# Vectors and weights laid out by partition in memory, an early tanh, and one count of landings for two DMA queues

## The chip, the core and the metric

The kernel runs on one core of a Trainium2 chip. The core has five engines with instruction streams of their own: TensorE (PE, with its weight loads in a row PEld), VectorE (DVE), ScalarE (ACT), GpSimd (POOL) and SyncE (SP). SP and ACT also issue DMAs: each has a queue in its own stream, and all of them are carried out by the same 16 DMA engines. The metric is device time in microseconds (us) of one execution; smaller is better.

## The reference, cut to what matters

One layer of a streaming encoder on 2048 prompt rows and 64 sample rows of width 1024, in float32:

```python
mod = silu(c) @ w_ada + b_ada                       # six vectors per sequence, from c
sh1, sc1, gt1, sh2, sc2, gt2 = split(mod, 6)
h = rms_norm(x, norm1_g) * (1 + sc1) + sh1
z = h @ w_in                                        # glu_a | glu_b | q | k | v | g_conv | g_attn
u = glu_a * sigmoid(glu_b)
conv_out = silu(layer_norm(depthwise31(u) + b_dw)) @ w_conv_out
q, k = rms_norm(q) * q_norm_g, rms_norm(k) * k_norm_g        # per head of 64
o = softmax(q k^T / 8 + rel_bias, in a band of 9 chunks of 64) v
x = x + gt1 * ((sigmoid(g_conv) * conv_out + sigmoid(g_attn) * (o @ w_attn_out)) @ w_o)
h2 = rms_norm(x, norm2_g) * (1 + sc2) + sh2
x = x + gt2 * ((silu(gate) * up) @ w_ffn_out)       # gate, up = split(h2 @ w_ffn_in)
```

Outputs are x of both sequences, the last 30 rows of u, and the new rows of k and v. The sample sequence also reads cached rows (`cache_k`, `cache_v`, `cache_conv`).

## The kernel before, in words

**Precision and slabs.** Each float32 operand of a matmul is split into a high part (`whi`, `hh`, `part_h`; an ACT copy to a shorter format) and a low part (`wlo`, `hl`, `part_l`; a subtraction on DVE or POOL), and a product is three matmuls: high by high, high by low, low by high (`mm3`). Weights come from memory in slabs of 512 KB into staging tiles (`wst`, three of them), are split into `whi` and `wlo`, and some split slabs are stored (`w_din_h`, `w_dqkv_h`, ...) to be read again in a later block.

**Stages.** The rows are worked on in four blocks of about 512. A block goes through q, k, v, four conv stages and the gates "g"; the attention of a block (scores `sc`, softmax in `pr` and `sm`, its transposed parts `ph` and `pl`, output `po`) runs beside the conv and gate products. In each gate step ACT makes a tile `gate` and stores it to `g_d` by a DMA in its own queue. The 31 taps of the convolution are DVE instructions on `y`. A second phase in three blocks does the two out-projections and the feed-forward network.

**The start** (`first_rows`, `setup`, `first_block`). The sums for c @ w_ada need `cl`, which is made from c by one tanh on ACT, and the slabs `wmod` of w_ada, four of which fit (`Slabs`). Before, c and the other vectors are read as rows (`r`) and turned into columns by PE. The rows `x_t` are squared on ACT, scaled by DVE after a power on POOL, turned by PE (`turn`, into `pt`), scaled by the modulation (`h`), split into `hh` and `hl`, and multiplied with the first slabs of w_in for q (`ps`).

**What sets the order.** No instruction is issued when the code calls it: `Plan.do` records it, and `Plan.flush` plays all engines forward with a table of costs and writes the instructions in the order of the planned starts. A DMA is planned no earlier than the landing of the eighth DMA before it (`Plan.room` with `self.flight`); which ready instruction comes first on an engine goes by a due time that is worked out backwards from the order of PE, with 8000 ns added to a DMA's latency.

**Semaphores of DMAs.** In the built program the DMAs of SP and ACT together take eight semaphores in turn, so a DMA of either queue waits at its issue until the eighth DMA before it, of whichever queue, has landed. What stands behind it in the stream of its engine waits with it, on ACT the activations too.

All instructions that are recorded in the plan carry line 388 in the profile, where `flush` issues them, so they are told apart by the names of their tiles.

Of the kernel before, what the change touches and what calls it, by code (L numbers as in the profile page):

```python
# [9 lines left out]
F32 = mybir.dt.float32  # L10
# [148 lines left out]
class Plan:  # L159
# [145 lines left out]
    def flush(self, last=False):  # L305
# [106 lines left out]
    def place(self, o, s):  # L412
# [534 lines left out]
def streaming_layer(ctx: ExitStack, tc: tile.TileContext, I, O):  # L947
# [7 lines left out]
    w_in, w_ada = I["w_in"][0], I["w_ada"][0]  # L955
    w_co, w_ao, w_o = I["w_conv_out"][0], I["w_attn_out"][0], I["w_o"][0]
    w_fi, w_fo = I["w_ffn_in"][0], I["w_ffn_out"][0]
# [3 lines left out]
    ck = I["cache_k"][0, 0].rearrange("t h d -> t (h d)")  # L961
# [31 lines left out]
    dve.memset(mhalf, -0.5)  # L993
# [7 lines left out]
    cols = const.tile([P, 76], F32, name="cols")  # L1001
    gates_c = const.tile([P, 2, 2, KT], F32, name="gates_c")
    lnh = const.tile([P, 8], F32, name="lnh")
    wd = const.tile([P, 4, TAPS], F32, name="wd")
    gqk = const.tile([P, 2], F32, name="gqk")
    gk = const.tile([P, HD], F32, name="gk")
    hist = const.tile([P, 4, HIST], F32, name="hist")
    hist_s = const.tile([P, 4, HIST], F32, name="hist_s")
# [5 lines left out]
    def source(key):  # L1014
        kind, a = key[0], key[1]
        by_col = lambda w, c0, n=P: w[:, c0 : c0 + n].rearrange("(k p) n -> p k n", p=P)
        if kind == "mod":
            if len(key) == 5:
                r = slice(512 * key[3], 512 * key[3] + 512)
                return [by_col(w_ada[r], a * D + key[2] * 2 * P, 2 * P)], 4, 2 * P  # L1020
            r = slice(256 * key[3], 256 * key[3] + 256)
            return [by_col(w_ada[r], a * D + key[2] * 512, 512)], 2, 512
        if kind == "qkv":
            r = slice(2 * key[2] * P, 2 * key[2] * P + 2 * P)
            return [by_col(w_in[r], 2 * CONV + 512 * a, 512)], 2, 512
        if kind == "in" and len(key) == 3:
            return [by_col(w_in[512 * key[2] : 512 * key[2] + 512], a, 2 * P)], 4, 2 * P
        if kind == "in":
            return [by_col(w_in, a)], KT, P
        if kind == "fi":  # L1030
            return [by_col(w_fi, a)], KT, P
        if kind == "up":
            return [
                sum_d[f][int(op[1]) - 1] if op[0] == "s"
                else by_col(w_fi[512 * (op != "a11") : 512 * (op != "a11") + 512], f * P + FFN * (op == "a22"))
                for f, op in key[1:]
            ], 4 * len(key) - 4, P
        if kind == "ca":
            return [by_col(w_co, a * P), by_col(w_ao, a * P)], KT, P
# [52 lines left out]

    plan.on = True
# [17 lines left out]
    def load_vectors():  # L1111

        r0 = temp("r0", (16, P))
        r1 = temp("r1", (76, P))
        by_row = lambda a: a.rearrange("(r c) -> r c", c=P)
        scalar.dma_start(r0[0:8], by_row(I["c_prompt"][0]))
        scalar.dma_start(r0[8:16], by_row(I["c_sample"][0]))
        yield r0, r1
        o = 0
        for name in ("norm1_g", "norm2_g", "b_dw", "conv_ln_g", "conv_ln_b", "b_ada"):  # L1120
            a = by_row(I[name][0])
            sync.dma_start(r1[o : o + a.shape[0]], a)
            o += a.shape[0]
        yield

    def setup():
        r0, r1 = first_vectors
        pt = ps_g.tile([P, 512], F32, tag="gp", name="pt")
# [17 lines left out]
        def vectors():  # L1146
            pt = ps_g.tile([P, 512], F32, tag="gp", name="pt")
            pe.transpose(pt[:, :76], r1, ident[:76, :76])
            dve.tensor_copy(cols, pt[:, :76])
# [5 lines left out]
        def taps():  # L1155
            for i in range(2):
                for j, g in enumerate((I["q_norm_g"], I["k_norm_g"])):
                    scalar.dma_start(gqk[HD * i : HD * i + HD, j : j + 1], g.rearrange("o d -> d o"))
            scalar.dma_start(gk, I["k_norm_g"].to_broadcast([P, HD]))
            cc = wk.tile([HIST, CONV], F32, tag="pr", name="cc", bufs=8)  # L1160
            scalar.dma_start(cc, I["cache_conv"][0, 0])
            r2 = wk.tile([TAPS, CONV], F32, tag="pr", name="r2", bufs=8)
            scalar.dma_start(r2, I["w_dw"][0])
            yield
            pt = ps_a.tile([P, 4, P], F32, tag="o", name="pt")
            for c in range(4):
                pe.transpose(pt[:, c, :TAPS], r2[:, c * P : (c + 1) * P], ident[:TAPS, :TAPS])
                pe.transpose(pt[:, c, 64 : 64 + HIST], cc[:, c * P : (c + 1) * P], ident[:HIST, :HIST])
            dve.tensor_scalar(wd, pt[:, :, :TAPS], 0.5, None, ALU.mult)
            dve.tensor_scalar(hist_s, pt[:, :, 64 : 64 + HIST], 2.0, None, ALU.mult)  # L1170
# [66 lines left out]
    def first_rows():  # L1237
        places = ((wa, "x", 3), (wa, "x", 3), (wa, "x", 3), (wk, "kk", 1), (wk, "q2", 1))
        queues = (sync, sync, scalar, sync, scalar)
        return [load_x(*tl, *place, q) for tl, place, q in zip(token_tiles(*PBLOCKS[0]), places, queues)]  # L1240

    def first_block(xs):
# [5 lines left out]
        def scale_rows(a, b):  # L1248
            for x_t, (t, n) in list(zip(xs, tiles))[a:b]:
                r = square(x_t, n)  # L1250
                dve.tensor_scalar(x_t[:n], x_t[:n], r, None, ALU.mult)

        def modulation(ct):
# [4 lines left out]
            with behind(pe.last.ins):  # L1258
# [88 lines left out]
    def store_kq(src, n, dst, col, g=None):  # L1347
# [4 lines left out]
        stream.after("act", "pe")  # L1352
        hi, lo = parts(shape=(P, 4, P))
# [60 lines left out]
    def cached_kv():  # L1414
        rows_ = [(src, j) for j in range(CACHE // P) for src in (ck, cv)]
        ts = []
        for i, (src, j) in enumerate(rows_):
            for src_, j_ in rows_[len(ts) : i + 2]:
                t = temp("cache")
                sync.dma_start(t, src_[j_ * P : (j_ + 1) * P])  # L1420
# [3 lines left out]
            if src is ck:  # L1424
                store_kq(t, P, k_d, j * P)
# [501 lines left out]
    vectors_ = load_vectors()  # L1927
    first_vectors = next(vectors_)
    M = Slabs(sync, scalar, wa, stream, list(mod_order()), source, 4)
    M.fill()  # L1930
    next(vectors_)
# [644 lines left out]
    "x_prompt", "x_sample", "c_prompt", "c_sample", "cache_conv", "cache_k", "cache_v", "norm1_g", "norm2_g",  # L2576
    "w_ada", "b_ada", "w_in", "w_dw", "b_dw", "conv_ln_g", "conv_ln_b", "w_conv_out", "q_norm_g", "k_norm_g",
    "rel_bias", "w_attn_out", "w_o", "w_ffn_in", "w_ffn_out",
# [4 lines left out]
]  # L2583

# [17 lines left out]
```

## Time and profile before

| | |
|---|---|
| median of three runs | 2958.19 us (2957.11 to 2959.2) |
| the profiled execution | 2954.55 us, its span 2952.7 us |
| PE busy | 2897.3 us, 98% of the span |
| DVE, ACT, POOL busy | 2056.5, 1361.9 and 1152.6 us |
| data moved by DMA | 628.06 MB, 213 GB/s over the span |

The span is the time from the first to the last instruction of the profiled execution. PE has work in 98% of it; the other 55.4 us are spread over a few places, which a list of waits names together with what ended each. "granted clock" (PEclk) is the share of full speed at which TensorE's clock ran in a stretch.

### The profile page before, as it was taken

Reading aid. Unit: us, or ns where it says so; the run is one execution under the profiler, and the core shown is the slowest. Engines: PE = TensorE matmul, PEld = TensorE weight load, DVE = VectorE, ACT = ScalarE, POOL = GpSimd, SP = SyncE. Lnnn points to the kernel's source line nnn. Section 1 sums busy time; section 2 is a strip of 40 time slices with the busy share of each in tenths; the row PEclk is TensorE's granted clock in tenths of the full one; section 3 lists DMA queues with packets and bytes.
Section 4 is the critical chain, followed back from the end, with each engine's and each line's share of the span. In section 5 each row is a group of like instructions: output and inputs, shape, how many; then the busy total and the mean of one; then the engine's idle time right before and its main releaser. Section 6 shows DMA issues by size and latency. Waiting matters only on the chain.

```text
span 2952.7 us, 44886 instructions
## 1 busy us (share of the span) xinstructions
PE 2897.3 (98%) x16241; PEld 2590.4 (88%) x16241; DVE 2056.5 (70%) x3628; ACT 1361.9 (46%) x2459; POOL 1152.6 (39%) x752
## 2 busy tenths in 40 slices
PE   7999999999999999989999999999999999999999
PEld 4899888888888888878888899999999999999998
DVE  5887788668867885577666745666666557576666
ACT  3345633662464356554444345544444355444442
POOL 0201310111011002544566452366666742465667
PEclk9999999999999999999999999999999999999999
DMA  9988999988886987975444876333333965333333
GB/s 293 300 296 289 300 308 317 297 261 315 278 280 201 314 259 237 312 258 169 145 143 143 265 248 225 108 117 97 105 122 111 335 221 185 97 104 104 115 110 123
DMA packets 467725, 628.06 MB, mean 213 GB/s; under 512 B 36277, under 2 KB 314665, under 8 KB 467502
## 3 DMA queue, kind: packets, MB, share of 16 engines
q1 hardware_dynamic: 453456, 605.58, 62.9%
q10 hardware_dynamic: 14045, 19.60, 1.9%
q8 instruction: 128, 2.10, 0.3%
q14 instruction: 96, 0.78, 0.1%
HBM read 476.53 MB, written 148.54 MB: 212 GB/s over the span
## 4 chain that ended last, share of the span: by engine, by line
PE 89%; DVE 4%; ACT 2%; DMA 2%; issue 1%; POOL 1%; SPq 0%; ACTq 0%; DVEq 0%; POOLq 0%
PE ps L388 59%; PE pd L388 16%; PE pw L388 6%; PE po L388 2%; PE sc L388 2%; PE ptp L388 2%; PE pt L388 1%; PE pa L388 1%; ACT whi L388 1%; DVE wlo L388 1%; DMA wst<-in_w_in 1%; DVE y L388 0%; POOL wlo L388 0%; DVE pw L388 0%; POOL ws L388 0%
## 5 line engine op out<-in xcount | busy, mean ns | idle before, releaser
L388 PE MATMUL ps<-t,whi 128*128 128x384 f32 (+1 forms) x2112 | 501.0, 322 | 8.9 <-ACT t L388 5.4
L388 POOL TENSOR_TENSOR wlo<-wst,whi 128x1024 fp32r<-128x1024 f32 (+1 forms) x160 | 365.2, 2291 | 292.9 <-ACT whi L388 243.8
L388 ACT ACTIVATE whi<-wst 128x1024 fp32r<-128x1024 f32 (+1 forms) x264 | 256.8, 976 | 292.0 <-PE ps L388 115.4
L388 PE MATMUL ps<-b,whi 128*128 128x384 f32 (+1 forms) x1584 | 381.9, 326 | 5.4 <-DVE t L388 2.2
L388 PEld LDWEIGHTS ps<-t,whi 128*128 128x128 f32 x2112 | 368.8, 188 | 15.4 <-ACT t L388 5.6
L388 DVE SCALAR_TENSOR_TENSOR y<-u,wd,y 128x512 f32<-128x512 f32 (+1 forms) x480 | 371.0, 775 | 7.8
L388 DVE TENSOR_TENSOR acc<-acc,pd 128x512 f32<-128x512 f32 (+1 forms) x482 | 324.4, 685 | 55.4 <-PE pd L388 49.7
L388 PE MATMUL ps<-hh,whi 128*128 128x512 f32 (+2 forms) x992 | 362.4, 366 | 0.0
L388 PE MATMUL ps<-hh,wlo 128*128 128x512 f32 (+2 forms) x992 | 346.6, 350 | 0.0
L388 PE MATMUL ps<-hl,whi 128*128 128x512 f32 (+2 forms) x992 | 346.1, 349 | 0.0
L388 PE MATMUL ps<-t,wlo 128*128 128x384 f32 (+1 forms) x1056 | 339.2, 322 | 0.0
L388 PE MATMUL pd<-whi,hid 128*128 128x512 f32 (+1 forms) x956 | 307.1, 391 | 0.0
L388 PEld LDWEIGHTS ps<-b,whi 128*128 128x128 f32 x1584 | 278.5, 189 | 11.6 <-DVE v L388 2.9
L388 PE MATMUL ps<-b,wlo 128*128 128x384 f32 (+1 forms) x792 | 257.3, 325 | 0.0
L388 ACT ACTIVATE pr<-pr,sm 128x640 f32<-128x640 f32 (+4 forms) x272 | 199.4, 746 | 119.8 <-DVE sm L388 114.5
L388 POOL TENSOR_TENSOR t<-t,mhalf 128x1 f32<-128x1 f32 (+3 forms) x68 | 85.9, 1270 | 425.5 <-DVE t L388 403.0
L388 PEld LDWEIGHTS pd<-whi,hid 128*128 128x128 f32 (+1 forms) x956 | 174.8, 183 | 40.9 <-ACT whi L388 0.2
L388 PEld LDWEIGHTS ps<-hh,wlo 128*128 128x128 f32 x992 | 187.4, 189 | 22.2 <-issue 0.9
L388 PEld LDWEIGHTS ps<-hh,whi 128*128 128x128 f32 x992 | 188.1, 190 | 18.4 <-issue 2.0
L388 PEld LDWEIGHTS ps<-hl,whi 128*128 128x128 f32 x992 | 188.4, 190 | 15.1 <-issue 1.2
L388 PEld LDWEIGHTS ps<-t,wlo 128*128 128x128 f32 x1056 | 198.5, 188 | 0.1
L388 POOL TENSOR_TENSOR wlo<-ws,whi 128x512 fp32r<-128x512 f32 x96 | 123.0, 1300 | 186.1 <-ACT whi L388 186.1
(232 smaller groups left out, 6297.6 us busy)
## 6 DMA issues: line engine op xcount, KB each, us to landing
whi<-w_din_h SPq DMA_DIRECT2D x72, 512.0 KB, 6.0
wlo<-w_din_l SPq DMA_DIRECT2D x72, 512.0 KB, 7.7
wst<-sum_d SPq DMA_DIRECT2D x132, 256.0 KB, 2.9
wfo<-in_w_ffn_out SPq DMA_DIRECT2D x64, 512.0 KB, 3.3
wmod<-in_w_ada SPq DMA_DIRECT2D x46, 512.0 KB, 6.1
sum_d<-ws SPq DMA_DIRECT2D x88, 256.0 KB, 2.6
wst<-in_w_ffn_in SPq DMA_DIRECT2D x84, 256.0 KB, 3.3
wst<-in_w_in SPq DMA_DIRECT2D x40, 512.0 KB, 8.9
```

Of the source, the lines that this page charges most:

```text
L388: f(*args, **kw)
```

## The change

It has four parts.

1. **Layout.** The host hands over the weights with the data of each slab contiguous for each partition (4 KB for one partition of a slab of 512 KB), all vectors as one tile of 128 x 92 with a column for each vector of 128 (`vec`), the taps, conv history and gains of q and k as one tile of 128 x 310 (`small`), and the cached k rows already turned. This only rearranges, repeats and joins arrays. Six loads of vectors, two of c, and seven small loads in `taps` become two loads; 18 transposes on PE and the copies behind them go; the two loads of a slab of conv and attention output weights (`ca`) become one.
2. **Start.** ACT issues the load of `vec` first, and a tanh of a constant right behind it, so that the table of functions is loaded while it lands. All slabs and all rows x are issued by SP; before, ACT issued two slabs and two rows. The square of a row is one instruction of 1024 elements, whose discarded result goes to the PSUM tile that `turn` uses first, instead of two of 512.
3. **Planner's flight.** `flight` is one list for both queues, as the semaphores are.
4. **Planner's due times.** 12000 ns in place of 8000 ns is added to a DMA's latency.

```diff
-        self.clock, self.pools, self.flight = 0.0, 0, {e: [] for e in ('sp', 'act')}
+        self.clock, self.pools, self.flight = 0.0, 0, []
...
-            lat = o.lat + self.HOP + (o.occ + o.size + 8000.0 if o.size else 0)
+            lat = o.lat + self.HOP + (o.occ + o.size + 12000.0 if o.size else 0)
...
-        if o.size and len(self.flight[o.engine]) > 7:
-            s = max(s, self.flight[o.engine][-8] + self.HOP)
+        if o.size and len(self.flight) > 7:
+            s = max(s, self.flight[-8] + self.HOP)
...
-            self.flight[o.engine].append(o.end)
+            self.flight.append(o.end)
...
-                return [by_col(w_ada[r], a * D + key[2] * 2 * P, 2 * P)], 4, 2 * P
+            return [I["ada_1"][a, key[2], key[3]]], 4, 2 * P
...
-            return [by_col(w_co, a * P), by_col(w_ao, a * P)], KT, P
+            return [I["w_ca"][a]], KT, P
...
+    scalar.dma_start(vec, I["vectors"])
+    act.activation(mhalf[:, 7:], eps_t, AF.Tanh)
+    dve.memset(mhalf, -0.5)
     plan.on = True
...
-        pe.transpose(pt[:, :16], r0, ident[:16, :16])
-        cc = wk.tile([P, 16], F32, tag="c0")
-        dve.tensor_copy(cc, pt[:, :16])
+        cc = vec[:, :16]
...
-            pe.transpose(pt[:, :76], r1, ident[:76, :76])
-            dve.tensor_copy(cols, pt[:, :76])
...
-                pe.transpose(pt[:, c, :TAPS], r2[:, c * P : (c + 1) * P], ident[:TAPS, :TAPS])
-                pe.transpose(pt[:, c, 64 : 64 + HIST], cc[:, c * P : (c + 1) * P], ident[:HIST, :HIST])
...
-        queues = (sync, sync, scalar, sync, scalar)
-        return [load_x(*tl, *place, q) for tl, place, q in zip(token_tiles(*PBLOCKS[0]), places, queues)]
+        return [load_x(*tl, *place) for tl, place in zip(token_tiles(*PBLOCKS[0]), places)]
...
-                r = square(x_t, n)
+                ssq = wk.tile([P, 2], F32, tag="ssq", name="ssq", bufs=3)
+                junk = ps_a.tile([P, 2 * 512], F32, tag="s", name="junk")
+                act.activation(junk[:n], x_t[:n], AF.Square, accum_out=ssq[:n, :1])
+                r = rsqrt_mean(wk, ssq[:n, :1], n, 1, D)
...
-            if src is ck:
-                store_kq(t, P, k_d, j * P)
+            if src == "k":
+                store_parts(t.rearrange("p (h t) -> p h t", h=4), P, k_d, j * P)
...
-    M = Slabs(sync, scalar, wa, stream, list(mod_order()), source, 4)
+    M = Slabs(sync, sync, wa, stream, list(mod_order()), source, 4)
...
+    a["ada_1"] = ada[:, : 2 * D].reshape(2, 4, P, 2, 4, 2 * P).transpose(3, 4, 0, 2, 1, 5)
+    a["w_gates"] = w_in[:, 2560:].reshape(2, 4, P, 8, 2 * P).transpose(3, 0, 2, 1, 4)
+    a["w_up"] = a["w_ffn_in"][0].reshape(KT, P, 2 * NF, P).transpose(2, 1, 0, 3)
```

The parts 3 and 4 change the order of instructions on all engines through the first phase and the beginning of the second. Two places are shown.

The first is ACT's stream from its first instruction, before. `r` holds the vector c, `rv` the table of relative biases, `t` the tanh of c, and `junk` the squares of the rows `x_t`:

```order
L388 DMA r_200<-in_c_prompt 8x128
L388 DMA r_200<-in_c_sample 8x128
L388 DMA wmod<-in_w_ada 128x4x256 x2
L388 DMA x_t<-in_x_prompt 128x1024 x2
L388 DMA rv<-in_rel_bias 8x257
L388 ACT_TABLE_LOAD
L388 ACTIVATE t<-t 128x16
L388 ACTIVATE junk,ssq<-x_t 64x512 x2
L388 ACTIVATE junk,ssq<-x_t 128x512 x8
L388 ACTIVATE whi<-wst 128x1024
```

And the same place in the changed kernel:

```order
L242 DMA vec<-in_vectors 128x92
L242 ACT_TABLE_LOAD
L242 ACTIVATE mhalf<-eps_t 128x1
L388 ACTIVATE t<-vec 128x16
L388 DMA rv<-in_rel_bias 8x257
L388 ACTIVATE junk,ssq<-x_t 64x1024
L388 ACTIVATE junk,ssq<-x_t 128x1024 x4
L388 ACTIVATE whi<-wst 128x1024
```

The tanh `t` moved from behind seven DMAs to behind one, and the load of the table from behind them to the place right after that one.

The second place is ACT's stream in the gates of block 0, beside the third head's scores, before. `pr` are the exponentials of the scores, 128 to 512 wide by chunk, `gate` the gate tiles, `whi` the high part of a slab:

```order
L388 ACTIVATE pr,sm<-pr,sm 128x256
L388 ACTIVATE gate<-ps 128x288
L388 ACTIVATE whi<-wst 128x1024
L388 ACTIVATE pr<-pr,sm 128x256
L388 ACTIVATE gate<-ps 128x288
L388 DMA g_d<-gate 128x288
L388 ACTIVATE pr,sm<-pr,sm 128x384
```

The same head's place in the changed kernel:

```order
L388 ACTIVATE pr,sm<-pr,sm 128x256
L388 ACTIVATE whi<-wst 128x1024
L388 ACTIVATE pr<-pr,sm 128x256
L388 ACTIVATE whi<-wst 128x1024
L388 ACTIVATE gate<-ps 128x288
L388 ACTIVATE pr,sm<-pr,sm 128x384
```

Between the exponentials of two chunks of one head stood one split of a slab, and now stand two; the store of a gate moved behind the next exponential. The loads of these slabs on SP's queue before, up to the first store of an attention output, `o_d` (`vv` are value rows, `w_din` stored slabs, `out` an output of the convolution state):

```order
L388 DMA vv<-v_d 128x4x128
L388 DMA out<-cc 30x128
L388 DMA wst<-in_w_in 128x4x256
L388 DMA w_din_1_h<-whi 128x1024
L388 DMA w_din_1_l<-wlo 128x1024
L388 DMA wst<-in_w_in 128x4x256
L388 DMA w_din_0_h<-whi 128x1024
L388 DMA vv<-v_d 128x2x128
L388 DMA vv<-v_d 64x128
L388 DMA w_din_0_l<-wlo 128x1024
L388 DMA o_d<-part_h 128x512
```

And in the changed kernel:

```order
L388 DMA vv<-v_d 128x4x128
L388 DMA wst<-in_w_gates 128x1024
L388 DMA w_din_1_h<-whi 128x1024
L388 DMA w_din_1_l<-wlo 128x1024
L388 DMA w_din_0_h<-whi 128x1024
L388 DMA w_din_0_l<-wlo 128x1024
L388 DMA vv<-v_d 128x2x128
L388 DMA vv<-v_d 64x128
L388 DMA out<-cc 30x128
L388 DMA o_d<-part_h 128x512
```

The last slab ahead of the output store is now issued six places ahead of `vv` 64x128 instead of three, and the conv state's store behind it.

More of the change, by code (lines that the diff above doesn't have):

```diff
@@ L1155, in taps @@
         def taps():
[L1156 to L1163, printed above, removed]
-            yield
-            pt = ps_a.tile([P, 4, P], F32, tag="o", name="pt")
-            for c in range(4):
-                pe.transpose(pt[:, c, :TAPS], r2[:, c * P : (c + 1) * P], ident[:TAPS, :TAPS])
-                pe.transpose(pt[:, c, 64 : 64 + HIST], cc[:, c * P : (c + 1) * P], ident[:HIST, :HIST])
-            dve.tensor_scalar(wd, pt[:, :, :TAPS], 0.5, None, ALU.mult)
-            dve.tensor_scalar(hist_s, pt[:, :, 64 : 64 + HIST], 2.0, None, ALU.mult)
+            scalar.dma_start(small, I["small"])
+            yield
+            dve.tensor_scalar(wd, wd, 0.5, None, ALU.mult)
+            dve.tensor_scalar(hist_s, hist_s, 2.0, None, ALU.mult)
         return vectors, taps, begun
@@ L1256, in modulation @@
             cs = [slice(c6 * 2 * P, (c6 + 1) * 2 * P) for c6 in range(2)]
-            with behind(pe.last.ins):
+            with behind(pe.last.ins) if ct else nullcontext():
                 for c6, c in enumerate(cs):
@@ L1414, in cached_kv @@
     def cached_kv():
-        rows_ = [(src, j) for j in range(CACHE // P) for src in (ck, cv)]
+        rows_ = [(src, j) for j in range(CACHE // P) for src in ("k", "v")]
         ts = []
@@ L2575 @@
 _INS = [
-    "x_prompt", "x_sample", "c_prompt", "c_sample", "cache_conv", "cache_k", "cache_v", "norm1_g", "norm2_g",
-    "w_ada", "b_ada", "w_in", "w_dw", "b_dw", "conv_ln_g", "conv_ln_b", "w_conv_out", "q_norm_g", "k_norm_g",
-    "rel_bias", "w_attn_out", "w_o", "w_ffn_in", "w_ffn_out",
+    "x_prompt", "x_sample", "cache_v", "rel_bias", "w_o", "w_ffn_out", "vectors", "small", "cache_k_t", "ada_1",
+    "ada_2", "w_qkv", "w_gates", "w_glu", "w_up", "w_ca",
 ]
@@ L2592 @@
     arrays, ins = {}, {}
-    for name in _INS:
-        a = np.ascontiguousarray(inputs[name])
+    for name, a in laid_out(np, inputs).items():
         arrays[f"in_{name}"] = a
```

74 lines of the change are left out of this document (34 added, 40 removed).

## The prediction

> **What bounds the kernel now.** I read the busy times first, then the waits of PE, then a table of stretches, and last the order of time at the places that these name.
>
> ```profile
> span 2952.7 us, 44886 instructions
> ...
> PE 2897.3 (98%) x16241; PEld 2590.4 (88%) x16241; DVE 2056.5 (70%) x3628; ACT 1361.9 (46%) x2459; POOL 1152.6 (39%) x752
> ...
> PE pa L388 <- DVE cl L388: 8.4, 1, 8.4
> PE sc L388 <- DVE sm L388: 8.1, 4, 3.2
> PE ps L388 <- ACT t L388: 5.4, 1, 5.4
> PE pt L388 <- DMA r<-in_c_sample: 4.8, 1, 4.8
> ```
>
> PE is idle for 2952.7 - 2897.3 = 55.4 us, and no matmul product is taken away. So the change can bring what is in those 55.4 us, the work of the transposes, and full clock where it runs slow. The waits (total, times, longest) put the largest pieces at the start (`cl`, `r`), in the attention (`sc`) and at the beginning of the feed-forward network (`t`).
>
> **The start.** In order of time (start, duration, instruction; in brackets the idle time before):
>
> ```profile
> 0.73 1.00 SPq L388 DMA_DIRECT2D wmod<-in_w_ada  x2
> ...
> 1.70 0.97 ACTq L388 DMA_DIRECT2D wmod<-in_w_ada  x2
> ...
> 6.10 0.34 SPq L388 DMA_DIRECT2D r<-in_b_ada  x1
> ...
> 11.09 0.30 ACTq L388 DMA_DIRECT2D rv<-in_rel_bias  x1
> ...
> 11.42 1.28 ACT L388 ACT_TABLE_LOAD   x1 [11.42 <-DMA wmod<-in_w_ada]
> 12.71 0.22 ACT L388 ACTIVATE t<-t 128x16 f32<-128x16 f32 x1
> 12.84 0.61 ACT L388 ACTIVATE junk<-x_t 64x512 f32<-64x512 f32 x1
> ...
> 13.40 3.64 PE L388 MATMUL pa<-wmod,cl 128*32 128x256 f32 x32 [8.38 <-DVE cl L388]
> ...
> 16.33 0.40 SPq L388 DMA_DIRECT2D wst<-in_w_in  x1
> ...
> 18.55 0.15 DVE L388 TENSOR_SCALAR t<-ssq 128x1 f32<-128x1 f32 x1
> ...
> 18.79 0.56 POOL L388 TENSOR_TENSOR t<-t,mhalf 128x1 f32<-128x1 f32 x1 [3.63 <-DVE t L388]
> ...
> 19.39 0.75 DVE L388 TENSOR_SCALAR x_t<-x_t,t 128x1024 f32<-128x1024 f32 x1 [0.68 <-POOL t L388]
> ...
> 25.41 0.67 DVE L388 TENSOR_SCALAR h<-pt,A,B 128x384 f32<-128x384 f32 x1
> ...
> 26.66 0.34 DVE L388 TENSOR_SCALAR h<-pt,A,B 128x64 f32<-128x64 f32 x1 [0.57 <-PE pt L388]
> ...
> 27.03 0.58 ACT L388 ACTIVATE hh<-h 128x448 fp32r<-128x448 f32 x1 [5.27 <-DVE h L388]
> ...
> 27.66 1.54 PE L388 MATMUL ps<-whi,hh 128*64 128x512 f32 x3 [1.04 <-ACT hh L388]
> ...
> 30.41 1.41 PE L388 MATMUL pt<-ident,x_t 64*128 64x64 f32 x5
> ...
> 32.18 2.09 PE L388 MATMUL pa<-wmod,cl 128*32 128x256 f32 x32
> ```
>
> The load of `rv` stands in ACT's stream ahead of the table load and the tanh. It waits for a semaphore that the first slab on ACT's queue holds, so the tanh runs only at 12.71 and the squares only from 12.84, although c was there by 4.8 us (the wait on `r`). The first product `ps` starts at 27.66; from then on PE has work.
>
> The load of `wst` at 16.33 waits for the last row x, so by then four slabs of 512 KB, four rows of 512 KB and one of 256 KB, 4.46 MB, are in.
>
> **Step 1, the start of the changed kernel.** Now c comes with `vec`, and the table is loaded meanwhile. I take 5 us for its landing (4.8 for c), and 5.4 for `cl`. The sums then go at the pace of the slabs, which come before the rows in one queue: 2.1 MB. The rate is read from a stretch in which only slabs and rows moved (columns: PE, PEld, DVE, ACT, POOL busy, granted clock, DMA share, GB/s):
>
> ```profile
> 12.00:14.00 2.00, 0.60 (x8) 0.37 (x12) 0.47 (x3) 1.99 (x6) 0.21 (x1) 1.00 1.06 374
> ```
>
> At 374 GB/s from 2 us on the fourth slab lands near 8 us, so modulation is ready before the rows and leaves the path. The last row lands between 2 + 4.46/0.374 = 13.9 and 16.3 as before; I take 15.3, nearer the old value, since half of the old loads were these same rows in 4 KB pieces. Behind it: a square of 1024 in one instruction, two of 0.61 less one start-up, some 1.2 (16.5). Its result goes to the PSUM tile of the first transposes, so these, which went ahead of it before, now wait for it: four at the cold pace of 1.41/5, 1.1 (17.6). Then `h` of 384 (0.67), the last row's scaling, which now follows it on DVE (0.75; its 0.15 and 0.56 lie beside the transposes), `h` of 64 (0.34), `hh` (0.58), and hops of 0.05 each: 20.2. Gain 27.66 - 20.2 = 7.4 us.
>
> What could be late next: the second four slabs. SP issues them behind the first `wst`, which waits for the landing of `rv`. The nearest row for a small load on a full queue is `b_ada`: 7.2 us from issue to landing.
>
> ```profile
> r<-in_b_ada SPq DMA_DIRECT2D x1, 24.0 KB, 7.2
> ```
>
> So `wst` goes out at 12.2; it and four slabs, 2.6 MB, land by 15.3 + 7.0 = 22.3. PE wants them 32.18 - 27.66 = 4.5 us behind the first product, at 24.7. They are 2.4 us early. The bounds: 8.8 us of gain with the row at 13.9; 6.4 with it at 16.3, and 4.8 if besides the last row's way through DVE and POOL, 18.55 to 20.14 in the rows above, comes on the path after all.
>
> The Trainium skill, DMA: Bandwidth & Descriptors (Specifications), gives 512 B as the smallest transfer for line rate, which speaks against the layout: slabs read in 1 KB runs would already be at full rate. By it the last row lands at 16.3 and step 1 is 6.4. The stretch at 374 GB/s agrees with it.
>
> **Step 2, the transposes.** Sixteen of the 18 stand behind the start (eight of cached k, four of taps, four of history). Four transposes on the chain of work take 0.44:
>
> ```profile
> 301.88 0.44 PE pt L388 x4
> ...
> 74.00:148.00 74.00, 73.63 (x427) 62.55 (x428) 65.53 (x100) 26.83 (x43) 21.34 (x18) 1.00 0.91 300
> 148.00:222.00 74.00, 74.00 (x515) 70.84 (x514) 66.12 (x115) 32.31 (x67) 1.64 (x4) 1.00 0.86 296
> ```
>
> 16 x 0.11 = 1.8 us, and PE is busy throughout the stretches where they stand, so all of it is on the path (at the other end 0, where PE would wait instead). The copies behind them on DVE and the 13 DMAs less are off the path; PE's work hides them. Table load 1.28 and tanh now lie in the wait for `vec`; if `vec` landed at once, they would cost 1.3 ahead of `cl`, which has 8 - 5.4 us to spare.
>
> **Step 3, the planner's order in the attention.** The wait of SP over the whole run, that of PE from 222 to 260 us with the place in time and the clock behind it, and that of PE from 333 to 370 with its clock:
>
> ```profile
> SPq L388 <- DMA g_d<-gate: 110.5, 34, 8.3
> ...
> PE sc L388 <- DVE sm L388: 3.2, 1, 3.2
> ...
> 235.10 1.32 SPq L388 DMA_DIRECT2D wst<-in_w_in  x1
> ...
> 241.80 1.06 ACT L388 ACTIVATE whi<-wst 128x1024 fp32r<-128x1024 f32 x1 [3.55 <-DMA wst<-in_w_in]
> ...
> 242.89 1.23 DVE L388 TENSOR_TENSOR wlo<-wst,whi 128x1024 fp32r<-128x1024 f32 x1 [1.96 <-ACT whi L388]
> ...
> 246.00:250.00 4.00, 4.00 (x17) 3.90 (x16) 3.96 (x9) 2.44 (x7) 0.00 (x0) 0.50 1.02 356
> 250.00:254.00 4.00, 4.00 (x28) 3.98 (x28) 1.84 (x3) 0.78 (x3) 0.00 (x0) 0.87 1.05 282
> ...
> PE sc L388 <- DVE sm L388: 3.7, 2, 2.9
> ...
> 340.00:344.00 4.00, 3.98 (x15) 3.41 (x16) 2.86 (x8) 2.42 (x6) 0.00 (x0) 0.60 1.06 369
> ```
>
> The queue of SP stands 110.5 us, 34 times, until a store of a gate has landed that ACT issued. The old planner counts eight DMAs for each queue and does not know of this. At 235.10 a slab goes out and lands near 241.8; ACT holds its `whi` 3.55 us, DVE its `wlo`, the softmax behind them is late, and PE waits 3.2 us for `sm`. Then the clock is granted at 0.50. From 333 to 370 us the same wait takes 3.7. Idle: 6.9 us. Clock lost: 0.5 x 4.0 + 0.13 x 4.0 + 0.4 x 4.0 = 4.1. In all 11.0.
>
> The new order knows the shared count, and issues the slab of this place some places earlier; but it puts two splits between the exponentials of one head, so a late slab still holds the scores. Nothing in the old trace shows the new waits. The ends are all 11.0 gained, or as much lost; I take half gained, 5.5, because the cause is one that the count addresses and the order around it is as tight as before.
>
> The Trainium skill, TensorE: Matmul & The Clock Gate (Part 1), has the clock fall to half after an idle window of about 3.4 us and return after as long a busy one. The stretch at 0.50 behind 3.2 us agrees. By that rule the clock's part comes back whole as soon as the waits are a little shorter: 3.4 of idle and 4.1, which would be 7.5 in place of 5.5.
>
> The 4000 ns more of due time and the layout I put at nothing of their own: DMAs are hidden behind PE from 74 us on, with a share of 0.86 to 0.91. If that cover went, the price is a rival below. The feed-forward start (5.4, `t`) waits for a backlog on ACT and DVE whose work stays; its order changes a little, and I put it at 0, between 5.4 gained and 5.4 lost.
>
> **The sum.** 7.4 + 1.8 + 5.5 = 14.7 us. The profiled execution took 2954.55 (span 2952.7), 3.6 under the median; it would take 2939.8. From the median, 2958.2 - 14.7 = 2943.5.
>
> **Rivals.** (a) All late waits in the attention go, and the start is worth 8.8: 8.8 + 1.8 + 11.0 = 21.6, 2936.6. For it speaks that all loads wait in SP's one queue; against it that PE waits at `sc` for a chain through four engines.
>
> (b) The start is given back. DMA is busy 0.86 to 0.91 up to 222 us. If PE comes 7 us earlier and the data doesn't, PE waits 7 us later on, and steps 2 and 3 leave 1.8 and some of the 5.5: 2951 to 2957, with 2954 in the middle. Against it: PE is busy 73.63 and 74.0 of 74 there, so data came ahead of need.
>
> (c) Slower: two splits in ACT's stream between the exponentials of a head. If slabs of the gates land as late as at 235 us, each such head costs 3.2 idle and 2.5 of clock, 5.7. The start and the transposes bring 9.2, so it decides from two such heads on, beside the one there was; with four more, 4 x 5.7 - 9.2 = 13.6: 2972. Against it: one head of eight in block 0 did so before.
>
> (d) The planner's parts don't do what they say, because other waits take the place of those on `g_d`: steps 1 and 2 alone, 9.2: 2949.0.
>
> **How the numbers follow.** A difference of 0.2%, 5.9 us, is about what a measurement of this kernel tells from no change. The forecast with its neighbourhood (2939 to 2947) has 0.45, (d) 0.2, (a) 0.14, (b) 0.14, (c) 0.07. Faster takes the forecast, (a), (d) less 0.02, and a little of (b): 0.8. Same takes most of (b) and the rest: 0.13. Slower is (c): 0.07. The range runs from 2934, below (a) by its own uncertainty of the clock, to 2957, the upper end of (b); it leaves out (c) and the tails of (a), together 0.15.
>
> **What would show it.** The first `ps` near 20 us and the tanh before 6; no idle of PE from there to 74; the wait for `cl` no longer the largest. SP's wait for `g_d` far under 110.5 us. The wait of `sc` for `sm` near 4 in place of 8.1, and fewer stretches with a clock under 1 between 222 and 370 us. Unchanged: the steady stretches from 1400 us on. I am wrong if the first product comes after 23 us, if PE waits for `wmod` or `wst` behind it, or if the attention of block 0 has more than one wait of 3 us.

## The result and the profile after

The changed kernel takes 2934.28 us (median of 4 runs, 2932.65 to 2939.12) beside 2957.65 for the kernel before (4 runs): a ratio of 0.9925, 95% interval 0.9907 to 0.9942. Measured again later, it took 2937.47 beside 2954.92, 0.9936 (0.9924 to 0.9949). So it is faster, by 23.4 us the first time and 17.5 the second; the forecast was 14.7. The first pair is the one forecast, and its profile, at 2932.65, is the one read here.

From the page of the kernel after, and then from its waits (total, times, longest) those of PE and SP's for stored gates:

```profile
span 2930.3 us, 44710 instructions
...
PE 2887.0 (99%) x16223; PEld 2579.8 (88%) x16223; DVE 2054.0 (70%) x3621; ACT 1362.2 (46%) x2450; POOL 1157.5 (39%) x752
```

```profile
PE ps L388 <- DVE t L388: 6.3, 2, 5.8
PE pa L388 <- DVE cl L388: 5.9, 1, 5.9
PE pt L388 <- ACT junk L388: 3.2, 1, 3.2
...
PE sc L388 <- DVE sm L388: 2.1, 2, 1.5
...
SPq L388 <- DMA g_d<-gate: 70.5, 30, 8.6
```

PE's idle time fell from 55.4 to 43.3 us (2930.3 - 2887.0): 12.1 of the 22.4 us that the span lost. The other 10.3 are PE's own busy time. By the places of the table below, 2.8 of it lie between the first product and 202 us, where most of the transposes stood, and 4.8 behind 1696 us, in the steady stretches, which the forecast left unchanged. `r` is gone, `sm` is down from 8.1 to 2.1, a new wait for `junk` (3.2) has come at the start, and the wait for `cl` (5.9) is still the longest single one.

The start of the kernel after in order of time, and then the table of the two stretches behind it:

```profile
1.18 1.28 ACT L242 ACT_TABLE_LOAD   x1 [1.18 <-PEq L2580]
...
5.25 0.21 ACT L388 ACTIVATE t<-vec 128x16 f32<-128x16 f32 x1 [2.57 <-DMA vec<-in_vectors]
...
11.40 1.02 ACT L388 ACTIVATE junk<-x_t 64x1024 f32<-64x1024 f32 x1 [5.94 <-DMA x_t<-in_x_sample]
...
14.49 0.16 DVE L388 TENSOR_TENSOR A<-A,vec 128x4 f32<-128x4 f32 x1
14.57 0.75 DVE L388 TENSOR_SCALAR x_t<-x_t,t 64x1024 f32<-64x1024 f32 x1
...
16.27 1.03 ACT L388 ACTIVATE junk<-x_t 128x1024 f32<-128x1024 f32 x1
...
17.47 1.36 PE L388 MATMUL pt<-ident,x_t 64*128 64x64 f32 x3 [3.21 <-ACT junk L388]
17.55 0.75 DVE L388 TENSOR_SCALAR x_t<-x_t,t 128x1024 f32<-128x1024 f32 x1 [0.67 <-POOL t L388]
...
19.02 0.75 DVE L388 TENSOR_SCALAR x_t<-x_t,t 128x1024 f32<-128x1024 f32 x1 [0.67 <-POOL t L388]
...
20.34 0.68 DVE L388 TENSOR_SCALAR h<-pt,A,B 128x384 f32<-128x384 f32 x1 [0.51 <-PE pt L388]
20.94 0.74 DVE L388 TENSOR_SCALAR x_t<-x_t,t 128x1024 f32<-128x1024 f32 x1
21.60 0.34 DVE L388 TENSOR_SCALAR h<-pt,A,B 128x64 f32<-128x64 f32 x1
...
22.60 1.54 PE L388 MATMUL ps<-whi,hh 128*64 128x512 f32 x3
```

```profile
74.00:148.00 74.00, 74.00 (x410) 62.17 (x409) 65.32 (x96) 24.34 (x39) 14.72 (x12) 1.00 0.89 311
148.00:222.00 74.00, 74.00 (x538) 71.90 (x537) 70.48 (x123) 35.77 (x75) 2.73 (x5) 1.00 0.86 289
```

The tanh runs at 5.25 in place of 12.71. Of `scale_rows`, each row's mean, power and scaling go DVE, POOL, DVE, and DVE takes up the next row only then: the scalings start at 14.57, 16.06, 17.55, 19.02 and, with `h` between, 20.94; the first four are 1.47 to 1.49 us apart, twice the 0.75 of a scaling.

This chain begins behind `A`, the scale that the modulation gives: its second instruction starts at 14.49, and the first scaling stands behind it in DVE's stream. The first product follows 8.11 us after it. In all seven kernels with this order of the start (after, measured twice, e2_raw, e3_perqueue, e6_unpad, e9_zero, e10_noplanner) the distance is 8.10 to 8.11 us, though `A` itself comes between 13.66 and 15.54; in the four with the old start it is 5.66 to 5.67. So what moves the first product from run to run is when `A` comes.

To see where the lead over the kernel before comes from, I set five places of the two traces side by side: the first product `ps`, the last `po` of 64x64 of the first short heads, the transpose of `gates_c` behind the attention, the first `ps<-cin` of 384 columns, and the end. The first product's rows stand above (27.66 and 22.60), and the end is the span; the other three, before and then after:

```profile
202.40 0.27 PE L388 MATMUL po<-pl,vv 64*128 64x64 f32 x1
1162.05 0.27 PE L388 MATMUL pt<-ident,gates_c 128*32 128x128 f32 x1
1695.92 0.52 PE L388 MATMUL ps<-cin,whi 128*128 128x384 f32 x2
```

```profile
194.14 0.27 PE L388 MATMUL po<-pl,vv 64*128 64x64 f32 x1
1147.87 0.27 PE L388 MATMUL pt<-ident,gates_c 128*32 128x128 f32 x1
1677.92 0.51 PE L388 MATMUL ps<-cin,whi 128*128 128x384 f32 x2
```

The differences give the lead at each place, and the differences of the leads what each part gained. The table has it in us for every kernel that was run, each against the same profile of before. The last column is explained with the first experiments:

| kernel | to the first product | to 202 us | attention, to 1162 | to 1696, start of the feed-forward network | to the end | halves |
|---|---|---|---|---|---|---|
| after | 5.1 | 3.2 | 5.9 | 3.8 | 4.4 | equal |
| after, second time | 4.9 | 3.1 | 1.2 | 3.6 | 4.2 | equal |
| e5_pad | 0.7 | 1.0 | -1.5 | -0.3 | 5.0 | equal |
| e6_unpad | 5.9 | 2.7 | 3.3 | 4.0 | -0.7 | mixed |
| e9_zero | 4.9 | 3.1 | 0.0 | 3.8 | 4.3 | equal |
| e1_layout | 1.6 | -0.5 | -0.8 | 0.4 | 0.1 | mixed |
| e2_raw | 4.0 | 3.3 | 6.2 | 4.3 | 4.1 | equal |
| e7_planner | 1.9 | -0.9 | 6.6 | 2.5 | -0.7 | mixed |
| e3_perqueue | 5.2 | 3.8 | -1.2 | 2.2 | 4.3 | equal |
| e10_noplanner | 5.4 | 1.2 | 4.5 | 0.0 | 4.4 | equal |
| e4_rows | 5.8 | 3.3 | 3.0 | 4.0 | 4.3 | equal |
| e11_twoq | 2.5 | 4.2 | 4.3 | 1.4 | 4.3 | equal |
| e12_rows2 | 7.0 | 0.3 | 2.0 | 3.6 | 4.3 | equal |

What was gained from 1696 us to the end repeats within 0.9 us in each of the two groups, equal and mixed. The attention's doesn't: one and the same program gained 5.9 and 1.2 there. e5_pad has the instructions and the order of before, and gains 0.7 and 1.0 in the first two parts. So single profiles settle the parts to 202 us and from 1162 to 1696 us within about 1 us, and the attention only within some 5 us.

### The profile page after: what moved, and what is told of

Read it like the earlier page. It is cut to its first block, busy times and chain, and to the rows that moved or that the text cites. A ratio compares the mean times of both kernels' runs of the same rounds, so it can differ in the third digit from the quotient of the medians.

```text
span 2930.3 us, 44710 instructions
## 1 busy us (share of the span) xinstructions
PE 2887.0 (99%) x16223; PEld 2579.8 (88%) x16223; DVE 2054.0 (70%) x3621; ACT 1362.2 (46%) x2450; POOL 1157.5 (39%) x752
## 3 DMA queue, kind: packets, MB, share of 16 engines
q10 hardware_dynamic: 12416, 17.55, 1.7%
## 4 chain that ended last, share of the span: by engine, by line
PE 91%; DVE 3%; ACT 2%; DMA 2%; issue 1%; POOL 1%; SPq 0%; ACTq 0%; DVEq 0%; POOLq 0%
PE ps L388 60%; PE pd L388 16%; PE pw L388 6%; PE po L388 2%; PE sc L388 2%; PE ptp L388 2%; PE pt L388 1%; PE pa L388 1%; DVE wlo L388 1%; ACT whi L388 1%; POOL wlo L388 0%; DVE pw L388 0%; POOL ws L388 0%; DVE t L388 0%; DMA tg<-g_d 0%
## 5 line engine op out<-in xcount | busy, mean ns | idle before, releaser
L388 DVE SCALAR_TENSOR_TENSOR y<-u,small,y 128x512 f32<-128x512 f32 (+1 forms) x480 | 370.3, 774 | 7.9
```

The source lines that it names most:

```text
L388: f(*args, **kw)
```

## Experiments: the places of the operands

The steady stretches gained, though PE does the same products in the same order there. In the chain of waits the runs of products between two pairs of projections read (start, duration, count), before and then after:

```profile
1940.11 20.93 PE ps L388 x120
...
1977.61 4.24 PE ps L388 x24
...
1983.93 20.93 PE ps L388 x120
```

```profile
1921.09 20.84 PE ps L388 x120
...
1958.51 4.16 PE ps L388 x24
...
1964.73 20.84 PE ps L388 x120
```

A pair takes 1983.93 - 1940.11 = 43.82 us before and 43.64 after. My first idea was the layout (below, theory L); it fell. Then I looked up where the built programs put the tiles, which no view of the profile shows. Before, the constants end so that the left pools (weights, `t`, `b22`, `hid`, half of `cin`) begin at multiples of 64 bytes in each partition, while the pool on the right side (`b11`, `b21`, the other half of `cin`) begins 32 bytes over. `vec` and `small` make the constants 32 bytes larger, and everything lies 32 over. The run of 24 consists of `b21` and `b11` alone, and the run of 120 has 24 of them.

e5_pad, on the kernel before:

```diff
     hist = const.tile([P, 4, HIST], F32, name="hist")
+    pad = const.tile([P, 8], F32, name="pad")
```

> The kernel before with one unused tile of 32 bytes per partition behind its constants, and nothing else: every engine's instructions and their order are those of before, but all tiles of the left pools (weights, t, b22, hid, half of cin) begin 32 bytes later. In the kernel before, these lie at multiples of 64 bytes, and b11, b21 and the other half of cin, on the right side, at 32 over; in the changed kernel both lie at 32 over, since its constants take 32 bytes more. Theory A (a product is some 4 ns longer where its two operands lie at different halves of 64 bytes, and the steady gain comes from the constants' new size): 43.63 us per pair of projections in place of 43.82, ps<-b,whi of 384 columns at 337 ns, and 5 to 8 us off the time of before. Rival B (the places mean nothing; the planner's new order of loads and of work on ACT, DVE and POOL does it): 43.82 us, time as before within 2 us.

Measured: 2949.73 us beside 2955.20, ratio 0.9981 (0.9972 to 0.9990): 5.5 us less, from a tile that nothing uses.

e6_unpad, on the changed kernel, and e9_zero, on e6_unpad:

```diff
-    eps_t = const.tile([P, 1], F32, name="eps_t")
...
-    small = const.tile([P, 310], F32, name="small")
+    small = const.tile([P, 312], F32, name="small")
+    eps_t = small[:, 310:311]
...
```

```diff
+    edge = rooms(ctx, name="edge", bufs=1, side="right")
+    edge.tile([P, 8], F32, name="edge")
     wa = rooms(side, name="wa", bufs=1, side="right")
```

> The changed kernel with its constants 32 bytes smaller (eps lies in the two spare columns of small), so that the left pools lie at multiples of 64 bytes again and b11, b21 and half of cin at 32 over, as in the kernel before. The order is the changed kernel's but for some hundred rows. Theory A: 43.82 us per pair, 5 to 8 us over the changed kernel's time, 2939 to 2942. Rival B: 43.63 us, within 2 us of 2934.

> As the kernel with the smaller constants, order and all, but the right pools begin 32 bytes lower too, so that all operands lie at multiples of 64 bytes. Theory A in the form that it is the difference between the two operands that costs: 43.63 us per pair, 5 to 8 us less than the kernel with the smaller constants. Theory A' (an operand of 384 columns that begins 32 bytes into 64 is slow by itself): also 43.63 here, but then the changed kernel, in which all operands begin so, could not be at 43.63. Rival B: no difference between the two.

Measured: e6_unpad 2942.68 (0.9957, 0.9944 to 0.9969), e9_zero 2937.42 (0.9941, 0.9928 to 0.9953). The chains of e5_pad, e6_unpad and e9_zero, in this order:

```profile
1939.26 20.84 PE ps L388 x120
...
1976.68 4.16 PE ps L388 x24
```

```profile
1924.18 20.93 PE ps L388 x120
...
1961.68 4.24 PE ps L388 x24
```

```profile
1927.38 20.84 PE ps L388 x120
...
1964.80 4.16 PE ps L388 x24
```

Theory A holds, in its first form: both operands at 0 or both at 32 is fast, mixed is slow, and A' and B fall. Mixed was always the same way round, the weights at 0 and the other operand at 32; the reverse was in no run. A control in the same traces are the products with `t`, which lies on the side of the weights: at 384 columns `ps<-t,whi` has a mean of 335 ns before, in e5_pad, e6_unpad, e9_zero and after, while `ps<-b,whi` goes from 339 before to 337 in e5_pad, back to 339 in e6_unpad and to 337 in e9_zero. The cost is 0.08/24 = 3.3 ns to 0.09/24 = 3.8 ns per product of 384 columns. There are 1440 mixed ones of that width (1056 with `b11` and `b21`, 384 with `cin`), so some 5 us, as e5_pad shows. Products of 288 columns show nothing: `ps<-b,whi` of that width has a mean of 300 ns before and in e5_pad.

The Trainium skill, TensorE: Matmul & The Clock Gate (Step-by-step: what each phase is for), says that the moving operand and the weights come through two independent read ports, so that loading weights takes nothing from a running product. By that the places of the two should not matter to each other; the runs of 24 differ by 0.08 us with them alone, so here they do. Which read waits isn't shown.

## Experiments: the layout

e1_layout, on the kernel before, and e2_raw, on the changed one, which undoes it for the weights of ada, in and up; in both the planner is told run lengths that keep the order as it was:

```diff
-            return [by_col(w_fi, a)], KT, P
+            return [I["w_up"][a // P]], KT, P
...
```

> The kernel before with one part of the change alone: the weights lie in memory by partition. The planner is given the old lengths of the runs, so every engine gets the instructions of the kernel before in its order; only the packets of the loads become fewer and longer. Theory L (the longer runs themselves shorten the work of PE: in the steady stretches one pair of up and down projections took 43.82 us before and 43.63 after, in the same order of products): 43.6 us per pair here too, the product ps<-b,whi of 384 columns at 337 to 338 ns in place of 340, and a time 4 to 8 us under that of the kernel before. Theory O (the new order of the loads and of the other engines does it, the layout nothing, as the prediction put it): 43.8 us per pair and a time within 2 us of before.

> The changed kernel with the projections' weights (ada, in, up) read from the matrices as they are given, in runs of 512 to 2048 bytes; the planner is given the new lengths of the runs, so every engine has the changed kernel's instructions in its order. The two output matrices, the vectors and the cached keys stay laid out. Theory L: 43.8 us per pair of projections in the steady stretches, a time 4 to 8 us over that of the changed kernel, 2938 to 2942. Theory O: 43.6 us per pair, within 2 us of 2934. At the start both expect the last row no earlier than in the changed kernel; if the slabs' short runs cost there, the first product comes later than 22.6 us.

Measured: e1_layout 2950.11 beside 2955.34, 0.9986 (0.9977 to 0.9995); e2_raw 2935.65, 0.9932 (0.9919 to 0.9946), between the two results of the changed kernel. The pairs, as a mean of seven, stay at 43.83 us in e1_layout and at 43.63 in e2_raw: theory L's reason is wrong, and the steady stretches don't depend on the packets. The time of e1_layout is nonetheless 5.2 us lower, as theory L had it and theory O had not; its profiled execution, at 2953.76 one of the slower ones, shows 0.8 of this, so where the rest lies is not shown. At the start, the first product of e2_raw comes at 23.65 us, 1.05 later than after, and PE begins the sums of its fourth slab as much later, at 10.71 in place of 9.66; in the other kernels with one queue and long runs that is 9.32 to 10.35. The 1.6 of e1_layout prove less, as e7_planner, in the old layout, has 1.9. After, then e2_raw, while hardly anything but slabs and rows was loaded:

```profile
3.00:5.00 2.00, 0.00 (x0) 0.00 (x0) 0.00 (x0) 0.00 (x0) 0.00 (x0) 1.00 0.98 390
5.00:7.00 2.00, 1.06 (x12) 0.55 (x16) 1.15 (x12) 0.21 (x1) 0.21 (x1) 1.00 1.02 418
```

```profile
3.00:5.00 2.00, 0.00 (x0) 0.00 (x0) 0.85 (x9) 0.21 (x1) 0.00 (x0) 1.00 1.05 368
5.00:7.00 2.00, 1.17 (x12) 0.32 (x16) 0.29 (x4) 0.00 (x0) 0.21 (x1) 1.00 1.09 349
```

Slabs in runs of 1 KB move at 349 to 368 GB/s, in long runs at 390 to 418. Over the whole of 3 to 7 us the nine kernels with the new start and long runs have 384 to 412, e2_raw 359; over 3 to 15 us it is 346 to 370 and 328. The rule of the Trainium skill, DMA: Bandwidth & Descriptors (Specifications), that 512 B are enough for line rate, does not hold in this stretch. The prediction put the layout at nothing for another reason, that the DMAs are hidden behind PE from 74 us on, and the time of e2_raw bears that out.

## Experiments: the planner

e7_planner is the kernel before with the shared count and the 12000 ns; e3_perqueue is the changed kernel without the shared count; e10_noplanner without either:

```diff
-        self.clock, self.pools, self.flight = 0.0, 0, []
+        self.clock, self.pools, self.flight = 0.0, 0, {e: [] for e in ('sp', 'act')}
...
-            lat = o.lat + self.HOP + (o.occ + o.size + 12000.0 if o.size else 0)
+            lat = o.lat + self.HOP + (o.occ + o.size + 8000.0 if o.size else 0)
```

> The kernel before with the planner's two changes alone (one count of landings over both queues, 12000 ns of due time), its own start, transposes, layout and places of tiles. Theory C (the planner takes the waits out of the attention and of the start of the feed-forward network): 4 to 9 us off the time of before, SP's wait for the stored gates at 60 to 75 us in place of 110, 43.82 us per pair in the steady stretches. Rival D (the attention gained by the earlier start and the loads' costs): within 2 us of before.

> The changed kernel with one part undone: the planner counts the eight landings for each queue apart, as before (due time and layout as in the changed kernel). Theory C (the shared count is what took the waits out of the attention): SP's wait for the stored gates goes back from 70 to some 110 us, PE's waits and the slow clock between 222 and 370 us come back, a time 4 to 7 us over the changed kernel's, 2938 to 2941. Rival D (the attention gained by other things that moved the order: the earlier start, the due time, the loads' new costs in the planner): within 2 us of 2934.

> The changed kernel with both of the planner's edits undone (landings counted for each queue, 8000 ns of due time); layout, start, transposes and places of tiles stay. Theory C (count and due time together bring the gain in the attention and most of that at the start of the feed-forward network): 6 to 10 us over the changed kernel, more than the kernel with the count alone undone; SP waits 95 to 115 us for stored gates. Rival D (the loads' new costs and the earlier start bring the attention's gain): within 3 us of the changed kernel. Rival E (the due time is worth nothing): as the kernel with the count alone undone, 3 to 5 us over.

Measured: e7_planner 2942.82 beside 2955.20, 0.9960 (0.9948 to 0.9973), 12.4 us less. But e3_perqueue 2938.35 (0.9940, 0.9927 to 0.9953) and e10_noplanner 2937.52 (0.9940, 0.9927 to 0.9953), beside 2934.28 and 2937.47 of the changed kernel: undoing the edits costs nothing that these intervals can tell. The 2938.35 of e3_perqueue lies in theory C's range, and in its trace the clock is granted below 1 in five stretches of 4 us between 222 and 370 us, as before, against two and three in the changed kernel; but e10_noplanner, which undoes more, has two and the changed kernel's time. The waits of e10_noplanner:

```profile
PE ps L388 <- ACT t L388: 5.4, 1, 5.4
...
PE sc L388 <- DVE sm L388: 1.7, 3, 1.0
...
SPq L388 <- DMA g_d<-gate: 104.2, 37, 9.3
```

SP waits 104.2 us for stored gates, nearly as before (110.5; with the edits 61.7 in e7_planner and 70.5 after), and yet `sm` costs PE 1.7 us, not 8.1. So SP's wait is not what held the scores. On the old kernel the planner's edits remove the late waits; on the changed one they are gone without them. Rival D is nearer, but which of the other parts does it (the earlier start, the loads' run lengths in the planner's costs, the missing transposes and DMAs) was not tried; e1_layout and e5_pad, which keep the old order, gained nothing there. The old wait for `t` of 5.4 us is back, and the lead at the start of the feed-forward network is 0.0 in place of 3.6 to 3.8. The changed kernel has a wait of 5.8 for another `t`, from DVE, in the same stretch; from 1260 to 1334 us PE waits 9.9 us before, 8.2 after and 9.6 in e10_noplanner, so the waits explain a part only. The edits seem to do something there, 2.2 of it without the count, but e11_twoq, with both edits, also has only 1.4.

## Experiments: the start

> The changed kernel itself, beside the three that follow. Both theories: 0.991 to 0.994 of the time of before, first product near 22.6 us, 43.63 us per pair.

That is the second result above: 0.9936, first product at 22.71.

e4_rows puts the mean of row i+1 ahead of the scaling of row i; e12_rows2 adds the columns `h` of four rows ahead of the fifth row's scaling, and `wlo` behind them; e11_twoq gives slabs and rows two queues again:

```diff
...
-                r = rsqrt_mean(wk, ssq[:n, :1], n, 1, D)
-                dve.tensor_scalar(x_t[:n], x_t[:n], r, None, ALU.mult)
+                late.append((x_t, n, rsqrt_mean(wk, ssq[:n, :1], n, 1, D)))
+                if len(late) > 1:
+                    with behind(dve.last.ins):
+                        scale(*late.pop(0))
...
```

```diff
-    M = Slabs(sync, sync, wa, stream, list(mod_order()), source, 4)
+    M = Slabs(sync, scalar, wa, stream, list(mod_order()), source, 4)
...
```

> The changed kernel with the scaling of the first rows written one row late: on DVE the mean of row i+1 stands ahead of the scaling of row i, so that DVE does not wait for POOL's power once per row. Theory S (the first product came at 22.60 and not at 20.2 because the rows go through DVE and POOL one after another, 1.47 us each, beyond the squares): last scaling ends near 19.2 in place of 21.7, first product at 20.3 to 20.9, 1.7 to 2.3 us earlier, and as much off the time, 2932, if the order that follows, which the planner makes anew, is as good. Rival R (the squares on ACT, 1.2 us each to 17.4, or the transposes behind them set it): first product not before 22.

> The changed kernel with the start put in another order on DVE: the mean of row i+1 ahead of the scaling of row i, the columns h of the first four rows ahead of the scaling of the fifth, and the first wlo behind these columns. Theory S (the way of the rows through DVE and POOL sets the first product): with the squares as before, the fourth row scaled at 18.5, h of 384 from 19.1, h of 64 to 20.1, hh to 20.7, first product at 20.7 to 21.0 in place of 22.6, and 1 to 2 us less time than the changed kernel, less than its runs differ among themselves. Rival R (the squares and transposes set it): not before 22.

> The changed kernel with slabs and first rows on two queues, SP's and ACT's, as before; vec, the table load and the first tanh stay ahead of them on ACT. Theory V (the start gained by c and the tanh coming first, not by the one queue): cl as early as in the changed kernel (near 5.7), first product within 0.7 us of 22.6. Rival Q (the one queue is needed, since a load in ACT's stream holds ACT's squares): the first square waits for the semaphore of an ACT load and the first product comes at 24 us or later, 2 us or more over the changed kernel's time.

Measured: e4_rows 2937.06 (0.9934, 0.9921 to 0.9947), e12_rows2 2938.52 (0.9944, 0.9932 to 0.9957), e11_twoq 2935.69 (0.9934, 0.9922 to 0.9947). e4_rows came to 21.84, between the theories, as `wlo` and the fifth row still stood ahead; e6_unpad came to 21.77 without this edit, so no gain of it is shown. `A` comes 0.7 to 0.8 us earlier in both than after. The start of e12_rows2:

```profile
13.29 0.16 DVE L388 TENSOR_TENSOR A<-A,vec 128x4 f32<-128x4 f32 x1
...
14.07 0.74 DVE L388 TENSOR_SCALAR x_t<-x_t,t 64x1024 f32<-64x1024 f32 x1
14.23 1.02 POOL L388 TENSOR_TENSOR t<-t,mhalf 128x1 f32<-128x1 f32 x1 [0.63 <-DVE t L388]
...
19.06 0.93 DVE L388 TENSOR_SCALAR h<-pt,A,B 128x384 f32<-128x384 f32 x2 [0.57 <-PE pt L388]
...
20.66 1.54 PE L388 MATMUL ps<-whi,hh 128*64 128x512 f32 x3 [1.63 <-ACT hh L388]
```

The place is theory S's: 20.66 us, with the squares where they were. But `A` comes 1.20 us earlier here than after (13.29 beside 14.49), mostly because PE took 0.71 us in place of some 1.22 for each of the two groups of products `pa<-sel,R` ahead of it. The distance from `A` to the first product fell from 8.11 to 7.37. By this count 1.2 of the 1.9 us come from `A` and 0.7 from the order of the rows; what that order gives with `A` where it is after was not run. And the 2 us are given back: at 202 us the lead is 7.3, under the 8.3 and 8.0 of the changed kernel, and the time is no better. In e11_twoq the first product comes at 25.12, as late as rival Q put it, but not for its reason, and the time is the changed kernel's. `rv` stands in ACT's stream again at 14.03 and a square behind it waits until 16.50; yet DVE takes the mean of the first row only at 16.28, behind `A` at 16.20, and needs that square's sum no earlier than 20.73. What is late are the sums: those of the fourth slab begin at 11.38 in place of 9.66. Of the kernels run, none is measurably faster than the changed one.

## Why the prediction was right, and where it was not

The sign was right, and so were the early tanh and, as far as it can be told, the work of the transposes. Of 22.4 us in the profile, 14.2 came from where the prediction looked (5.1, 3.2 and 5.9), and 8.2 from two places that it had put at nothing; the second time it was 9.2 (4.9, 3.1 and 1.2) and 7.8. The measured 2934.28 lies at the lower end of the range from 2934 to 2957. That it lies inside, and that 14.2 came so near 14.7, is in part luck.

**The start: 7.4 forecast, 5.1 measured.** The tanh (before 6) and `cl` were right, and so was that the transposes wait for the last square. It ended at 17.42 and not at 16.5, because the five squares run one behind another from 11.40 on, 1.2 us each. Two things failed. The modulation was to be ready before the rows and leave the path; its `A` came at 14.49, and the chain to the first product starts there. And in that chain I put only one scaling (0.75) behind the last square, and took the means and powers as lying beside the transposes. They don't, as DVE waits for POOL in each row; the row that showed it (18.55 to 20.14) was quoted, and used for the lower bound only. e12_rows2 takes these waits away and gets 20.66, 0.5 from the 20.2 that the step forecast, but 1.2 of its 1.9 us come with an earlier `A`. The first product, at 22.60, stayed only 0.4 under the 23 us from which the step would have been wrong, and the wait for `cl` stayed the longest single one (5.9 beside 5.8 for `t`), which the list had otherwise.

**The transposes: 1.8.** The part to 202 us, in which they stand, gained 3.2 and 3.1. PE is busy 74.00 of 74 there, as the step required, so all of them should count; but no run has them alone, the same part gained 1.0 in e5_pad with every transpose in place, and 1.2 in e10_noplanner without them. The price of 0.11 us each is too high for eight of the sixteen, those of the taps and the history, which start 0.06 to 0.09 us apart from 73.26 to 73.72 in the trace of before. What the other 1.3 is wasn't tried. Rival (b), the start given back, did not come.

**The attention: 5.5 forecast, 5.9 and 1.2 measured.** The size is within the scatter, so that 5.9 came so near 5.5 is luck, and the reason is not shown. I reasoned from SP's wait for the gates to the late slab to `sm`; e10_noplanner has that wait and not its consequence. Three items of the list also fit (`sm` 2.1 in place of 8.1, `g_d` 70.5, fewer stretches with a clock under 1), which shows how little a list of signs proves when one change moves the whole order. No wait of 3 us is left there, so rival (c) did not come.

**The feed-forward start: 0 forecast, 3.8 and 3.6 measured.** This stood inside its bounds of 5.4. The kernel without the planner's edits gains 0.0 there; what in the order brings it is not shown.

**"Unchanged: the steady stretches".** This was wrong: 4.4 us. The prediction costed what the change does to loads, waits and orders, and not that new constants move every tile behind them. It was visible beforehand, in the sizes of `vec` and `small`, but no trace of before could price it.

So the sum fell short by these 8.2, the transposes' 1.4 and the attention's 0.4, less the start's 2.3: 7.7, which is 22.4 - 14.7. Rival (a), 2936.6, is nearer to the time, but not for its reason.

## What to carry to other kernels

When an edit changes the size of anything allocated early, look at where the operands of the bounding products lie afterwards, and test that by itself with an unused tile. A change that moves a greedy planner's whole order must be undone part by part before its gain is put down to the part that was meant: here the two edits were worth 12.4 us on the old kernel and nothing measurable on the new one. And where an engine does a short step between two of another engine, row after row, count the round trip for each row, and not once. Where the way from one instruction to another takes the same time in every run, as from `A` to the first product, look at what moves the first before a gain is put down to an edit behind it.

## What the runs showed of the hardware

- A product of 384 columns whose two operands begin at different halves of 64 bytes (weights at 0, the other at 32) starts its successor 3.3 to 3.8 ns later; over 1440 of them 5 us of 2955. At 288 columns nothing showed.
- From 3 to 7 us, loads in runs of 1 KB reached 349 to 368 GB/s, in long runs 390 to 418, with a DMA share of 0.98 or more in both.
- POOL's power on 128x1 took 0.56 us while DVE waited for it, and 1.00 to 1.02 where a scaling of DVE ran beside it (14.07 to 14.81 above), so that taking DVE's wait away gave a part of it back to POOL.
